# Zeros in the bias tiles: bias and maximum of a score tile by one VectorE instruction

## The chip, the cores and the metric

The kernel runs on one core of a Trainium2 chip. The metric is the time of one execution on the device, in microseconds (us). TensorE (PE) does the matrix products, and its weight loads are listed as PEld; VectorE (DVE) and ScalarE (ACT) do the elementwise work, GpSimd (POOL) some of it, and SyncE (SP) issues most of the DMA transfers. Each engine, and each engine's DMA queue, takes its instructions in order.

## The reference

One step of a two-layer transformer on 128 context tokens and 512 latent tokens, in fp32. A layer has four parallel token mixers (A to D), gates, an output projection, and a gated MLP. Branch A is the one that is changed here: neighbourhood attention with a bias for each pair of positions.

```python
bias = rpb[:, dr[:, None, :], dc[None, :, :]]
s_loc = jnp.einsum('brqhd,brkhd->bhrqk', qg, kg) * scale + bias[None]
s_loc = jnp.where(col_ok[None, None, None], s_loc, NEG_INF)
s_ctx = jnp.einsum('brqhd,blhd->bhrql', qg, k_ctx) * scale
p = jax.nn.softmax(jnp.concatenate([s_ctx, s_loc], axis=-1), axis=-1)
o = (jnp.einsum('bhrql,blhd->brqhd', p[..., :L], v_ctx)
     + jnp.einsum('bhrqk,brkhd->brqhd', p[..., L:], vg))
```

So a query's softmax runs over its local keys, with bias, and over the 128 context keys, without.

## The kernel before

Every matrix product is done with fp32 operands split into two parts, a high part `H` and the rest `L`, and three products (high by high, low by high, high by low). Weights come through SP in pieces of up to 128x1024 (`raw`), are split by ACT into `wh` (line 303) and by DVE into `wl` (line 332), and feed accumulations that are called `d`. The operands of attention are called `c` and `g` (large slots), scores and small products stand in four PSUM tiles `ps`, attention outputs in `po`, probabilities in `p`.

The program is written out by a planner (`run`, from line 438). Each step is a Python generator; the planner keeps a clock for each engine (`clk`, line 229) with a cost for each instruction, and takes the next step that its clocks call ready, by priority; when none is, it lets TensorE go on with the dense products in the fixed list `fq`. What is written out is then the fixed order in which each engine does its work. A changed cost or a missing instruction therefore moves other instructions too, on all engines, as far as the mixer part of a layer goes.

Attention of a pair of heads has two passes. `attn1` (line 1783) makes scores with queries on the partitions, only to get each query's maximum and the sum of its exponentials. `attn2` (line 1908) makes the scores again with keys on the partitions, takes the exponential and multiplies with the values. Ahead of both, `prep64` splits and transposes queries and keys ("the K split" and "the K transposes" below: `split_l` at line 1584, and the products with `identR` at line 1593 and after).

In branch A, `attn1` has for each head one tile for the context queries and four tiles `b` of 128 latent queries. The latent tile holds 128 context keys and then 256 local keys (`b` of 0 and 3) or 384 (`b` of 1 and 2). Line 1801 adds the bias to the local part and takes its maximum (on the chip two instructions, CUSTOM_DVE_ANT_0 and a read of its accumulator), line 1804 takes the maximum of the 128 context columns, line 1813 joins both and negates, and ACT takes the exponential (line 303). There are 2 layers, 2 pairs, 2 heads and 4 tiles: 32 such tiles.

The bias tiles are loaded by SP (`bias_load`, line 1777) from arrays that the host lays out (`rpb0` for `attn1`, `rpb1` for `attn2`): for each head a load of 640 columns and one of `BIAS_W[which]` columns. In both layers the `rpb0` loads of the two pairs stand among weight loads, in the first layer also among the loads of `w_ada`, whose products with the condition (line 347, `c<-c,cs,c`) DVE sums for the modulation. Queries and keys of branches B to D that were computed early are stored to DRAM (`sp`) and loaded again ahead of their preparation (`restore`, line 1171).

Of the kernel before, what the change touches and what calls it, by code (L numbers as in the profile page):

```python
# [14 lines left out]
OP = mybir.AluOpType  # L15
AX = mybir.AxisListType

DEPTH = 2
# [89 lines left out]
AB1 = 1  # L108
MGQ = 1
RING = 10  # L110
BIAS_W = (256, 640)
WPOS = 6
XPOS = ((0, 1), (2, 3), (4, 5), (6, 7))

# [74 lines left out]
def emit(nc, tc, t):  # L189
# [18 lines left out]
    class S:  # L208
# [4 lines left out]
        w = NW  # L213
# [12 lines left out]
    def free(k, n=1):  # L226
        FREE[k] += [S.cur] * n

    def clk(e, cost, port=False):
        s = max(C[e], S.cur)  # L230
        if port:
            s = max(s, C["X"])
            C["X"] = s + cost - (130 if e == "G" else 0)
        C[e] = s + cost
        S.cur = s + cost + S.t[0]
# [30 lines left out]
    def SM(cols, dt=F):  # L266
        if cols > 10:
            return sp.tile([128, 32], dt, tag="r", name=nm("r"), bufs=5)[:, :cols]
        return sp.tile([128, 10], dt, tag="s", name=nm("s"))[:, :cols]

    def SL(cols):
        return sp.tile([128, 20], F, tag="sl", name=nm("sl"), bufs=6)[:, :cols]
# [40 lines left out]
    def vec(cols, port=False):  # L313
        clk("V", 67 + 1.042 * cols, port)
# [34 lines left out]
    def vsmall(n=1):  # L349
        clk("V", 90 * n)  # L350
# [105 lines left out]
    def has(*flag):  # L456
        return lambda: flag in done
# [1313 lines left out]
    def bias_load(l, p, which):  # L1771
        yield 4
        rows = [[Q(), Q()], [Q(), Q()]]
        for h in range(2):
            c0 = 0
            for b, w in zip(rows[h], (640, BIAS_W[which])):
                nc.sync.dma_start(b[:, :w], t["rpb%d" % which][l, p, h][:, c0:c0 + w])
# [5 lines left out]
    def attn1(l, br, p, res, idx):  # L1783
        terms = res["terms"]
        band = br in "AC"
        if br == "A":
            yield has("b", l, p, 0)
            bias1 = BIAS.pop((p, 0))
        NM = SL(10).rearrange("p (h j) -> p h j", h=2)
        S2 = SL(20).rearrange("p (h j x) -> p h j x", h=2, j=5)  # L1790
        nc.vector.memset(S2, 0.0)
        sk = [nsink[:, 2 * p + h:2 * p + h + 1] for h in range(2)] if br == "C" else None
        left = [0]

        def rest(h, j, ss, n, bt):
            mc = SM(2)
            s = ss[0]
            nmx = NM[:, h, j:j + 1]
            if bt is not None:
                vec(n)  # L1800
                nc.vector.tensor_tensor_reduce(out=s[:, 128:128 + n], in0=s[:, 128:128 + n], in1=bt, scale=1.0, scalar=-3e38,
                                               op0=OP.add, op1=OP.max, accum_out=mc[:, 0:1])
                vec(128)
                nc.vector.tensor_reduce(mc[:, 1:2], s[:, 0:128], axis=AX.X, op=OP.max)
                ex = [s[:, 0:128 + n]]
            else:
                ex = [x[:, :n] for x in ss]
                for x, e in enumerate(ex):
                    vec(n)
                    nc.vector.tensor_reduce(nmx if len(ex) == 1 and sk is None else mc[:, x:x + 1], e, axis=AX.X, op=OP.max, negate=True)  # L1810
            if bt is not None:
                vsmall()
                nc.vector.tensor_scalar(nmx, mc[:, 0:1], mc[:, 1:2], -1.0, op0=OP.max, op1=OP.mult)
            elif len(ex) == 2 or sk is not None:
                vsmall()
                nc.vector.tensor_scalar(nmx, mc[:, 0:1], mc[:, 1:2] if len(ex) == 2 else sk[h], None, op0=OP.min)
            yield
            for x, e in enumerate(ex):
                act(e, e, AF.Exp, bias=nmx, accum_out=S2[:, h, j, x:x + 1])
            free("s", len(ss))  # L1820
            left[0] += 1

        for h in range(2):
            tl = terms[h]["l1"]
            for j in range(5):
                two = j > 0 and not band
                yield N(s=2 if two else 1, at=S.pe)
                ss = [PS() for _ in range(1 + two)]
                bt = None
                qs = slice(128 * j, 128 * j + 128)  # L1830

                def score(o, a, b, last=True):
                    for i, (q, k, K) in enumerate(tl):
                        mm(o, q[0:K, qs], k[0:K, a:b], i == 0, last and i == len(tl) - 1)

                if j == 0:
                    n = 128
                    score(ss[0][:, 0:128], 0, 128)
                elif two:
                    n = 320  # L1840
                    for x in range(2):
                        score(ss[x][:, 0:320], 128 + 320 * x, 448 + 320 * x)
                else:
                    b = j - 1
                    lo, hi = max(b - 1, 0), min(b + 2, 4)
                    n = 128 * (hi - lo)
                    s = ss[0]
                    if lo:
                        score(s[:, 0:128], 128, 256)
                        score(s[:, 128:128 + n], 256 + 128 * lo, 256 + 128 * hi, br == "A")  # L1850
                    else:
                        score(s[:, 0:128 + n], 128, 256 + n, br == "A")
                    if br == "A":
                        X, Y = bias1[h]
                        bt = (X[:, 0:256], X[:, 256:640], X[:, 256:640], Y[:, 0:256])[b]
                    else:
                        ms = [(kb, 2 * (kb > b)) for kb in (b - 1, b + 1) if lo <= kb < hi]
                        for kb, w in ms:
                            mm(s[:, 128 + 128 * (kb - lo):256 + 128 * (kb - lo)], identR, maskR[:, 64 * w:64 * w + 128], False, (kb, w) == ms[-1])
                        n += 128  # L1860
                spawn(rest(h, j, ss, n, bt), 2)
        yield lambda: left[0] == 10

        if br == "A":
            for row in bias1:
                rel(*row)
        lse = SM(10)
        l2 = lse.rearrange("p (h j) -> p h j", h=2)
        vsmall()
        nc.vector.tensor_tensor(l2, S2[:, :, :, 0], S2[:, :, :, 1], op=OP.add)  # L1870
        if sk is not None:
            es = SM(10)
            e2 = es.rearrange("p (h j) -> p h j", h=2)
            sr = gain(l, "sink_c")[:, 2 * p:2 * p + 2]
            for h in range(2):
                act(e2[:, h], NM[:, h], AF.Exp, bias=sr[:, h:h + 1])
            yield
            vsmall()
            nc.vector.tensor_tensor(lse, lse, es, op=OP.add)
        ln = SM(10)  # L1880
        yield
        act(ln, lse, AF.Ln)
        yield
        nl = SM(10)
        n2 = nl.rearrange("p (h j) -> p h j", h=2)
        vsmall(12)
        nc.vector.tensor_tensor(n2, NM, ln.rearrange("p (h j) -> p h j", h=2), op=OP.subtract)
        for h in range(2):
            zH, zL = LZ[:, :, 32 * h], LZ[:, :, 32 * h + 1]
            nc.vector.tensor_copy(zH, n2[:, h])  # L1890
            nc.vector.tensor_tensor(zL, n2[:, h], zH.bitcast(F), op=OP.subtract)
        yield N(s=2)
        s, s2 = PS(), PS()
        for j in range(4):
            mm(s[0:34, j * 128:(j + 1) * 128], LZ[:, j + 1], identR, True, True)
        mm(s2[0:34, 0:128], LZ[:, 0], identR, True, True)
        for h in range(2):
            q, r0 = terms[h]["lse"]
            evac(q[r0:r0 + 2, 128:640], s[32 * h:32 * h + 2, :], False)
        free("s")  # L1900
        for h in range(2):
            q, r0 = terms[h]["lse"]
            evac(q[r0:r0 + 2, 0:128], s2[32 * h:32 * h + 2, 0:128], False)
        free("s")
        yield
        done.add(("lse", l, idx))
# [263 lines left out]
def _host(x_prompt, x_sample, cache_nat_k, cache_nat_v, cache_gqa_k, cache_gqa_v, cache_win_k, cache_win_v,  # L2170
# [13 lines left out]
    vec = np.zeros((DEPTH, 128, NV), np.float32)  # L2184
    for l in range(DEPTH):
# [7 lines left out]
                                axis=1).astype(np.float32)  # L2193
# [5 lines left out]
    idx = np.arange(16)[:, None] * -1 + 15 + np.arange(48)[None, :]  # L2199
    off = 7 - np.arange(8)[:, None] + np.arange(8)[None, :]  # L2200
    lay = lambda v: v[:, :, off][..., idx].transpose(0, 1, 2, 4, 3, 5).reshape(DEPTH, 2, 2, 128, 8, 48)
    for w, seq in enumerate((((1, 1), (2, 0), (0, 0), (1, 0), (2, 0), (0, 0), (1, 2)),
                             ((1, 1), (2, 0), (0, 0), (1, 0), (2, 0), (0, 0), (1, 0), (2, 0), (0, 0), (1, 2)))):
        tb = [lay(v[..., ::-1, ::-1] if w else v) for v in pads]
        a["rpb%d" % w] = np.ascontiguousarray(np.concatenate(
            [tb[v][..., 16 * d:16 * d + 16].reshape(DEPTH, 2, 2, 128, 128) for d, v in seq], axis=-1))
    a["cos64"], a["sin64"] = _rope(64)
    a["cos32"], a["sin32"] = _rope(32)
    a["maskC"] = _masks()
# [26 lines left out]
```

## Time and profile before

| | |
|---|---|
| median of 3 runs | 2325.96 us (2325.31 to 2327.69) |
| the profiled execution: time, span | 2329.46 us, 2327.7 us |
| busy in the span | PE 98%, PEld 94%, DVE 77%, ACT 48%, POOL 13% |
| mean granted clock of TensorE | 0.991 |
| bytes moved by DMA | 292.18 MB, 126 GB/s in the mean |

The span is the time from the first to the last instruction of that execution; the time itself lies 1.8 us above it. Clocks are given as a share of full speed: 1.00 is 2.4 GHz, 0.50 is 1.2 GHz.

### The profile page before, as it was taken

How to read it: one execution, taken by the hardware profiler on the slowest of the kernel's cores; microseconds unless marked ns; L12 is line 12 of the kernel's file. 1: busy time of each engine (PE TensorE's matmuls, PEld its weight loads, DVE VectorE, ACT ScalarE, POOL GpSimd, SP SyncE). 2: the span in 40 equal slices, each digit the busy share in tenths (PEclk: the TensorE clock that was granted, in tenths of full speed). 3: DMA queues.
4: the chain of work that ended last, by engine and by line, in shares of the span. 5: the costliest groups of instructions: out<-in, count | busy, mean ns of one | idle time of the engine just before them, and what ended most of it. 6: DMA issues, size and time to landing. Idle time of an engine off the chain costs nothing.

```text
span 2327.7 us, 40730 instructions
## 1 busy us (share of the span) xinstructions
PE 2273.9 (98%) x15480; PEld 2195.2 (94%) x15480; DVE 1800.1 (77%) x3399; ACT 1125.4 (48%) x2419; POOL 300.1 (13%) x563
## 2 busy tenths in 40 slices
PE   8899999999999999999999999999999999999999
PEld 3899999999999999999999989999999999999999
DVE  5678878878779888766677788887879997565566
ACT  4467767664344323233355676666534542323232
POOL 0112112312021000000022121132111200000000
PEclk9999999999999999999999999999999999999999
DMA  7632323335554342322264332233456432221313
GB/s 255 235 122 73 112 82 110 100 127 175 196 186 137 105 155 93 125 78 68 87 202 155 121 114 82 87 111 109 145 179 225 172 114 85 85 74 59 98 51 132
DMA packets 114018, 292.18 MB, mean 126 GB/s; under 512 B 15840, under 2 KB 24736, under 8 KB 113824
## 3 DMA queue, kind: packets, MB, share of 16 engines
q1 hardware_dynamic: 105664, 258.43, 33.8%
q0 software_dynamic: 8160, 31.15, 3.6%
q8 instruction: 122, 2.00, 0.4%
q14 instruction: 72, 0.59, 0.1%
HBM read 257.59 MB, written 31.95 MB: 124 GB/s over the span
## 4 chain that ended last, share of the span: by engine, by line
PE 76%; DVE 13%; ACT 4%; DMA 3%; issue 3%; SPq 0%; POOL 0%; DVEq 0%; ACTq 0%; POOLq 0%
PE d L368 63%; PE ps L368 10%; DVE c L347 3%; PE po L368 2%; DVE wl L332 2%; DMA c<-w_ada 2%; DVE c L332 1%; ACT wh L303 1%; DVE p L347 1%; DVE hL L347 1%; DVE g L332 1%; ACT ps L303 1%; DMA g<-sp 1%; ACT c L325 1%; ACT c L303 0%
## 5 line engine op out<-in xcount | busy, mean ns | idle before, releaser
L368 PE MATMUL d<-hH,wh 128*128 128x320 f32 x2432 | 760.4, 313 | 0.4 <-ACT hH L303 0.4
L368 PE MATMUL d<-hL,wh 128*128 128x320 f32 x2432 | 754.7, 310 | 3.4 <-DVE hL L347 3.4
L368 PE MATMUL d<-hH,wl 128*128 128x320 f32 x2432 | 753.9, 310 | 0.8 <-DVE wl L332 0.8
L368 PEld LDWEIGHTS d<-hL,wh 128*128 128x128 f32 x2432 | 460.1, 189 | 7.6 <-DVE hL L347 5.0
L368 PEld LDWEIGHTS d<-hH,wh 128*128 128x128 f32 x2432 | 459.9, 189 | 4.1 <-ACT hH L303 0.7
L368 PEld LDWEIGHTS d<-hH,wl 128*128 128x128 f32 x2432 | 459.5, 189 | 1.1 <-DVE wl L332 1.1
L303 ACT ACTIVATE wh<-raw 128x1024 fp32r<-128x1024 f32 (+4 forms) x344 | 333.7, 971 | 206.2 <-PE d L368 178.4
L368 PE MATMUL d<-c,wh 128*128 128x320 f32 x1776 | 411.5, 311 | 2.8 <-DVE c L347 1.1
L332 DVE TENSOR_TENSOR wl<-raw,wh 128x1024 fp32r<-128x1024 f32 (+4 forms) x344 | 383.4, 1115 | 35.1 <-ACT wh L303 33.0
L303 ACT ACTIVATE c<-d 128x320 f32<-128x320 f32 (+2 forms) x376 | 130.7, 372 | 389.6 <-PE d L368 384.2
L368 PEld LDWEIGHTS d<-c,wh 128*128 128x128 f32 x1776 | 300.6, 189 | 7.8 <-DVE c L347 2.2
L368 PE MATMUL d<-c,wl 128*128 128x320 f32 x960 | 297.1, 309 | 0.0
L368 PE MATMUL d<-wh,hH 128*128 128x256 f32 (+1 forms) x720 | 208.7, 290 | 3.9 <-ACT wh L303 2.4
L347 DVE SCALAR_TENSOR_TENSOR c<-c,cs,c 128x512 f32<-128x512 f32 x266 | 198.0, 791 | 15.9 <-DMA c<-w_ada 15.9
L368 PE MATMUL d<-wh,hL 128*128 128x256 f32 (+1 forms) x720 | 205.1, 285 | 3.4 <-DVE hL L347 3.4
L368 PE MATMUL d<-wl,hH 128*128 128x256 f32 (+1 forms) x720 | 205.3, 285 | 1.0 <-DVE wl L332 1.0
L303 ACT ACTIVATE c<-c 128x641 f32<-128x641 f32 (+8 forms) x197 | 127.8, 665 | 161.1 <-DVE c L347 78.4
L368 PEld LDWEIGHTS d<-c,wl 128*128 128x128 f32 x960 | 180.9, 188 | 0.0
L347 DVE SCALAR_TENSOR_TENSOR c<-c,vec,c 128x641 f32<-128x641 f32 x174 | 154.6, 888 | 12.7 <-DVE c L347 0.5
L368 PE MATMUL d<-g,wh 128*128 128x320 f32 x656 | 158.9, 309 | 0.0
L1337 DVE TENSOR_SCALAR c<-c,vec 128x641 f32<-128x641 f32 x87 | 53.5, 614 | 124.7 <-ACT c L303 121.5
L368 PEld LDWEIGHTS d<-wh,hH 128*128 128x128 f32 x720 | 138.1, 192 | 5.1 <-ACT wh L303 2.6
(196 smaller groups left out, 3449.2 us busy)
## 6 DMA issues: line engine op xcount, KB each, us to landing
raw<-wst SPq DMA_DIRECT2D x264, 512.0 KB
c<-w_ada SPq DMA_DIRECT2D x184, 256.0 KB
mgd<-c POOLq DMA_DIRECT2D x46, 320.0 KB, 3.2
raw<-wst SPq DMA_DIRECT2D x32, 320.0 KB
c<-mgd SPq DMA_DIRECT2D x30, 320.0 KB
raw<-wst SPq DMA_DIRECT2D x32, 256.0 KB
c<-rpb SPq DMA_DIRECT2D x24, 320.0 KB
c<-xin SPq DMA_DIRECT2D x16, 320.0 KB
```

Source lines behind the costliest of these rows:

```text
L303: nc.scalar.activation(out, in_, func, **kw)
L325: nc.scalar.copy(out, in_)
L332: nc.vector.tensor_tensor(out, a, b, op=op)
L347: nc.vector.scalar_tensor_tensor(out, a, s, b, op0=op0, op1=op1)
L368: nc.tensor.matmul(out, lhsT, rhs, start=start, stop=stop, skip_group_check=True)
L1337: nc.vector.tensor_scalar(y[:, :641], u[:, 1:642], c[:, 1:2], c[:, 3:4], op0=OP.mult, op1=OP.add)
```

## The change

The bias tiles of `attn1` get 128 columns of zeros beside the local ones, so that one instruction covers the whole score tile, local and context columns together. The load of 256 columns becomes one of 512. In the last tile (`b` of 3) the scores are written with the local keys first, so that the bias tile's zeros lie at its end. The reduction at line 1804 goes, and the small instruction that joined two maxima only negates one. The planner is told another cost for the long instruction.

```diff
-BIAS_W = (256, 640)
+BIAS_W = (512, 640)
...
             if bt is not None:
-                vec(n)
-                nc.vector.tensor_tensor_reduce(out=s[:, 128:128 + n], in0=s[:, 128:128 + n], in1=bt, scale=1.0, scalar=-3e38,
-                                               op0=OP.add, op1=OP.max, accum_out=mc[:, 0:1])
-                vec(128)
-                nc.vector.tensor_reduce(mc[:, 1:2], s[:, 0:128], axis=AX.X, op=OP.max)
+                e = s[:, 0:128 + n]
+                clk("V", 237 + 1.042 * (n + 128))
+                nc.vector.tensor_tensor_reduce(out=e, in0=e, in1=bt, scale=1.0, scalar=-3e38, op0=OP.add, op1=OP.max,
+                                               accum_out=mc[:, 0:1])
                 ex = [s[:, 0:128 + n]]
...
             if bt is not None:
                 vsmall()
-                nc.vector.tensor_scalar(nmx, mc[:, 0:1], mc[:, 1:2], -1.0, op0=OP.max, op1=OP.mult)
+                nc.vector.tensor_scalar(nmx, mc[:, 0:1], -1.0, None, op0=OP.mult)
...
-                    if lo:
+                    if br == "A" and b == 3:
+                        score(s[:, 0:n], 256 + 128 * lo, 256 + 128 * hi, False)
+                        score(s[:, n:128 + n], 128, 256)
+                    elif lo:
                         score(s[:, 0:128], 128, 256)
                         score(s[:, 128:128 + n], 256 + 128 * lo, 256 + 128 * hi, br == "A")
...
-                        bt = (X[:, 0:256], X[:, 256:640], X[:, 256:640], Y[:, 0:256])[b]
+                        bt = (X[:, 256:640], Y[:, 0:512], Y[:, 0:512], X[:, 0:384])[b]
...
-    for w, seq in enumerate((((1, 1), (2, 0), (0, 0), (1, 0), (2, 0), (0, 0), (1, 2)),
+    for w, seq in enumerate((((0, 0), (1, 2), None, (1, 1), (2, 0), None, (0, 0), (1, 0), (2, 0)),
...
-            [tb[v][..., 16 * d:16 * d + 16].reshape(DEPTH, 2, 2, 128, 128) for d, v in seq], axis=-1))
+            [np.zeros((DEPTH, 2, 2, 128, 128), np.float32) if e is None else
+             tb[e[1]][..., 16 * e[0]:16 * e[0] + 16].reshape(DEPTH, 2, 2, 128, 128) for e in seq], axis=-1))
```

TensorE's products are the same in number and size. Their order changes in the mixer part of both layers; from the output projection to the end of the MLP it is the same as before. Three places matter below. Line numbers after the change are up to 3 higher, and buffer numbers differ.

DVE in the first layer, at the loads of `w_ada`. Before:

```order
L332 TENSOR_TENSOR wl_831<-raw_728,wh_815 128x1024
L347 SCALAR_TENSOR_TENSOR c_582<-c_585,cs,c_582 128x512
L347 SCALAR_TENSOR_TENSOR c_583<-c_585,cs,c_583 128x512
L332 TENSOR_TENSOR wl_873<-raw_744,wh_859 128x1024
L347 SCALAR_TENSOR_TENSOR c_582<-c_586,cs,c_582 128x512
L347 SCALAR_TENSOR_TENSOR c_583<-c_586,cs,c_583 128x512
```

The same place with the change:

```order
L332 TENSOR_TENSOR wl_831<-raw_731,wh_815 128x1024
L332 TENSOR_TENSOR wl_870<-raw_747,wh_859 128x1024
L347 SCALAR_TENSOR_TENSOR c_582<-c_585,cs,c_582 128x512
L347 SCALAR_TENSOR_TENSOR c_583<-c_585,cs,c_583 128x512
L347 SCALAR_TENSOR_TENSOR c_582<-c_586,cs,c_582 128x512
L347 SCALAR_TENSOR_TENSOR c_583<-c_586,cs,c_583 128x512
```

The second weight split now stands ahead of the instruction that waits for a load of `w_ada` (into `c_585`), not behind it. A copy of 128x128 (`c_545<-d_818`) also comes to DVE, right behind these rows.

DVE some ten rows later, up to the K split of the first pair (`g_1073`, with the change `g_1065`). Before:

```order
L332 TENSOR_TENSOR wl_1004<-raw_833,wh_985 128x1024
L332 TENSOR_TENSOR c_996<-c_582,c_995 128x512
L332 TENSOR_TENSOR c_998<-c_583,c_997 128x512
L332 TENSOR_TENSOR g_438<-g_438,s_993 128x640
L332 TENSOR_TENSOR g_438<-g_438,gain_428 128x640
L332 TENSOR_TENSOR g_1035<-g_546,g_1035 128x6x64
L332 TENSOR_TENSOR g_1036<-g_546,g_1036 128x6x64
L332 TENSOR_TENSOR c_437<-c_437,s_1014 128x640
L332 TENSOR_TENSOR c_437<-c_437,gain_428 128x640
L332 TENSOR_TENSOR wl_1092<-raw_875,wh_1049 128x1024
L332 TENSOR_TENSOR g_1073<-g_438,g_1073 128x6x64
```

With the change:

```order
L332 TENSOR_TENSOR wl_1000<-raw_833,wh_985 128x1024
L332 TENSOR_TENSOR g_438<-g_438,s_980 128x640
L332 TENSOR_TENSOR g_438<-g_438,gain_428 128x640
L332 TENSOR_TENSOR c_437<-c_437,s_990 128x640
L332 TENSOR_TENSOR c_437<-c_437,gain_428 128x640
L332 TENSOR_TENSOR g_1027<-g_546,g_1027 128x6x64
L332 TENSOR_TENSOR g_1028<-g_546,g_1028 128x6x64
L332 TENSOR_TENSOR wl_1084<-raw_872,wh_1043 128x1024
L332 TENSOR_TENSOR g_1065<-g_438,g_1065 128x6x64
```

The two splits of the modulation's sums (`c_996`, `c_998`) are gone from here; they stand behind the K split now.

SP in the first layer, at the second pair's `rpb1` loads and the reload of branch B's first pair (`sp`). Before:

```order
L580 DMA raw_1821<-wst 128x544
L1013 DMA g_1894<-cache_win_k 128x64
L1014 DMA g_1894<-cache_win_v 128x64
L1777 DMA c_1908<-rpb 128x640
L1777 DMA c_1909<-rpb 128x640
L1777 DMA c_1910<-rpb 128x640
L1777 DMA c_1911<-rpb 128x640
L1171 DMA c_1916<-sp_1338 128x640
L1171 DMA g_1918<-sp_1340 128x768
L580 DMA raw_1944<-wst 128x816
```

With the change:

```order
L580 DMA raw_1778<-wst 128x544
L1013 DMA g_1862<-cache_win_k 128x64
L1014 DMA g_1862<-cache_win_v 128x64
L580 DMA raw_1882<-wst 128x816
L1777 DMA c_1978<-rpb 128x640
L1777 DMA c_1979<-rpb 128x640
L1777 DMA c_1980<-rpb 128x640
L1777 DMA c_1981<-rpb 128x640
L1171 DMA c_1986<-sp_1357 128x640
L1171 DMA g_1988<-sp_1359 128x768
```

A weight load has moved ahead of these six loads. In the second layer this place has the same order as before.

## Rows read from the trace of the kernel before

**Rows 1.** The page's busy time of each engine, share of the span, instructions

```profile
PE 2273.9 (98%) x15480; PEld 2195.2 (94%) x15480; DVE 1800.1 (77%) x3399; ACT 1125.4 (48%) x2419; POOL 300.1 (13%) x563
```

**Rows 2.** Groups by form, DVE: operation, shapes, count | busy us, mean ns | idle before

```profile
L1804 DVE TENSOR_REDUCE s<-ps 128x1 f32<-128x128 f32 x32 | 9.3, 292 | 1.1
...
L1801 DVE CUSTOM_DVE_ANT_0 ps<-ps,c 128x384 f32<-128x384 f32 x16 | 8.9, 557 | 0.1
...
L1801 DVE CUSTOM_DVE_ANT_0 ps<-ps,c 128x256 f32<-128x256 f32 x16 | 6.8, 425 | 0.3 <-ACT wh L303 0.3
```

**Rows 3.** Timeline of DVE, one bias tile, first layer: start us, us, instruction [idle before]

```profile
171.76 0.56 DVE L1801 CUSTOM_DVE_ANT_0 ps<-ps,c 128x384 f32<-128x384 f32 x1
172.24 0.14 DVE L1801 DVE_READ_ACCUMULATOR2_ANT s<- 128x1 f32 x1
172.41 0.29 DVE L1804 TENSOR_REDUCE s<-ps 128x1 f32<-128x128 f32 x1
172.74 0.21 DVE L1813 TENSOR_SCALAR sl<-s 128x1 f32<-128x1 f32 x1
172.87 0.42 DVE L332 TENSOR_TENSOR p<-p,p 128x256 fp32r<-128x256 f32 x1
```

**Rows 4.** Timeline of DVE, its first idle times around 191 us

```profile
167.29 1.01 DVE L332 TENSOR_TENSOR wl<-raw,wh 128x816 fp32r<-128x816 f32 x1 [0.58 <-ACT wh L303]
...
192.99 0.69 DVE L328 CAST g<-ps 64x512 fp32r<-64x512 f32 x1 [0.57 <-ACT g L325]
```

**Rows 5.** Timeline of PE: waits in the mixer part [idle before <-releaser]

```profile
76.06 0.38 PE L368 MATMUL d<-wh,hH 128*128 128x256 f32 x1 [2.38 <-ACT wh L303]
...
77.32 0.38 PE L368 MATMUL d<-wl,hH 128*128 128x256 f32 x1 [0.76 <-DVE wl L332]
...
108.39 0.66 PE L368 MATMUL ps<-identR,g 128*128 128x128 f32 x4 [3.18 <-DVE g L332]
...
129.56 0.73 PE L368 MATMUL ps<-g,c 66*128 66x512 f32 x2 [0.41 <-ACT ps L303]
...
191.66 0.55 PE L368 MATMUL ps<-identR,g 128*128 128x128 f32 x3 [0.99 <-DVE g L332]
...
1326.12 0.66 PE L368 MATMUL ps<-identR,g 128*128 128x128 f32 x4 [0.94 <-DVE g L332]
```

**Rows 6.** Windows: us, PE busy (matmuls), granted clock, DMA share, GB/s

```profile
70.00:72.00 2.00, 2.00 (x20) 1.00 0.74 215
72.00:74.00 2.00, 1.68 (x15) 1.00 1.00 397
76.00:78.00 2.00, 1.18 (x7) 1.00 1.02 401
108.40:116.40 8.00, 8.00 (x55) 0.79 0.22 68
232.00:246.00 14.00, 12.06 (x63) 0.76 0.57 186
1366.00:1378.00 12.00, 9.54 (x53) 0.86 0.54 188
```

**Rows 7.** Timeline of SP's DMA issues, first layer: start us, us to issue

```profile
65.07 2.10 SPq L1777 DMA_DIRECT2D c<-rpb  x4
...
80.47 1.85 SPq L1777 DMA_DIRECT2D c<-rpb  x4
...
163.11 1.85 SPq L1777 DMA_DIRECT2D c<-rpb  x4
...
168.33 20.05 SPq L580 DMA_DIRECT2D raw<-wst  x2
```

**Rows 8.** Timeline of DVE, first layer, up to the K split

```profile
89.89 1.41 DVE L347 SCALAR_TENSOR_TENSOR c<-c,cs,c 128x512 f32<-128x512 f32 x2 [3.96 <-DMA c<-w_ada]
91.22 1.22 DVE L332 TENSOR_TENSOR wl<-raw,wh 128x1024 fp32r<-128x1024 f32 x1
...
101.30 1.30 DVE L332 TENSOR_TENSOR c<-c,c 128x512 fp32r<-128x512 f32 x2
...
107.78 1.02 DVE L332 TENSOR_TENSOR g<-g,g 128x384 fp32r<-128x384 f32 x2
```

## Prediction

> **What bounds the kernel now.** I read the page's busy times first: TensorE is busy for 2273.9 of 2327.7 us [rows 1]. It does the same products after the change, so all that the change can win or lose is in the other 53.8 us, and in how often the clock falls. The second view was the difference between the two programs: the order of work moves only in the mixer part of the layers, so the idle time in the norms, in the output projection and in the MLP stays. The third was the timeline of TensorE in the mixer parts, for each wait and its releaser [rows 5]. These are single waits of 0.3 to 3.2 us, most of them released by DVE. The fourth was DVE's timeline ahead of those waits, and the fifth the granted clock behind them [rows 6].
>
> DVE is busy for 77% of the span in the mean, which would say that it bounds nothing. The stage says otherwise. In the first layer DVE works without a pause from 167.29 to 191.66 [rows 4], through the eight bias tiles of the second pair, and at 191.66 TensorE has waited 0.99 for DVE's split of the next pair's keys. At 1326.12, in the second layer, the same wait is 0.94 [rows 5]. A shorter tile ends these waits sooner.
>
> **The tile.** In the timeline, one tile's long instruction and the read of its accumulator take from 171.76 to 172.41, the reduction with its wait until 172.74, and the next work starts at 172.87 [rows 3]. The change takes out 172.74 - 172.41 = 0.33. It adds 128 columns to the long instruction: 557 - 425 = 132 ns for 128 columns [rows 2]. So a tile gets 0.33 - 0.13 = 0.20 shorter, eight tiles 1.6, all 32 6.3 us of DVE. A form with 512 columns isn't in the trace; that the slope goes on is taken from the two forms that are. If the widest form cost as much more as the whole reduction (292 ns), the tile would save 0.04, which is the lower bound. The last small instruction reads one operand less; I count nothing for it. Nothing else in the step changes on ACT: the exponential has the same columns. TensorE's products for the last tile come in another order, at the same count, and cost nothing.
>
> What lies on the path is less than 6.3. At 191.66 and 1326.12 TensorE can win only what it waits there, 0.99 and 0.94, since 1.6 is more than either; after that it has work again. At 129.56 it waits 0.41 for the exponential of a bias tile of the first pair [rows 5]; three tiles stand ahead of it, worth 0.6, so 0.41 goes. In the second layer's first pair TensorE doesn't wait in this way, and its shorter tiles are worth 0. Sum of the tiles: **-2.34**.
>
> **The larger loads.** Each of the two `rpb0` groups gets 2 x 128 x 256 x 4 bytes = 262 kB more, with no more instructions on SP. The second layer has room. In the first layer the groups at 65.07 and 80.47 [rows 7] stand in a queue that is behind: from 72 to 78 us the transfers run at a share of 1.00 and about 400 GB/s [rows 6]. At 397 GB/s a group costs 0.66, at the 215 of 70 to 72 us it costs 1.22. I take 0.66 for the weights behind the first group, whose wait ends in the fast stretch. TensorE's wait ahead of 76.06 grows from 2.38 to 3.0. By itself that is not lost, because at 108.39 TensorE waits 3.18 again, for the K split [rows 5], and what it comes later it waits less there.
>
> So the start is decided by DVE's chain to the K split. It begins with a wait of 3.96 for a load of `w_ada`, at 89.89, and goes on nearly without a pause to the first half of the split at 107.78 [rows 8]. By the order shown above, one weight split of 1.2 now runs ahead of that wait, the two splits at 101.30, together 1.3, run after the chain, and a copy of 128 columns comes in, about 0.3 by the reduction of the same size [rows 2, 8]. That is -2.2. The load itself lands later by both groups: 1.3 to 2.4. The chain ends 0.9 sooner to 0.2 later; I take 0.5 sooner, since the nearer row is the faster one, but the group's own loads ran in the slower one. TensorE comes 0.66 later, so of its 3.18 a wait of 3.18 - 0.66 - 0.5 = 2.0 is left.
>
> Behind the wait of 3.18 the granted clock is 0.79 for 8 us, so part of this time ran at 1.2 GHz; that costs (1 - 0.79) x 8 = 1.68. Behind 2.38 it stays at 1.00 from 76 to 78 [rows 5, 6]. The wait that is left is nearer to 2.38, so I take the fall as gone. Sum of the start: -0.5 - 1.68 = **-2.2**. The Trainium skill (TensorE: Matmul & The Clock Gate, section HAM oscillation — how this bites in real kernels) describes a kernel that waits for a load in each step and restarts at the lower clock every time. By that rule the start would win only 0.5, and the whole 2.9 instead of 4.5. The trace agrees for the wait of 3.18 and does not for that of 2.38.
>
> **The sum** is -2.34 - 2.2 = -4.5. The profiled execution took 2329.46, which would become 2325.0; it was 3.5 above the median of the runs, so against the median of 2325.96 the forecast is **2321.4**. That is 0.2% (4.65 us), about what a measurement of this kernel can tell from no change.
>
> **The rivals.**
>
> *More goes.* The order of the mixer part is written anew, with a cost for the long instruction that fits the chip. The waits where the last input projections end, from 232 to 246 and from 1366 to 1378, may go too. In the second of these TensorE is idle for 12.00 - 9.54 = 2.46 and the clock costs 0.14 x 12 = 1.68 [rows 6]. For it: these waits are released by DVE and ACT in stages where DVE is the busier one. Against it: the same small products and the same weights meet there in any order. With one of the two gone: 2321.4 - 4.1 = 2317.3.
>
> *The clock falls all the same.* Short waits can add up: from 232 to 246 the clock is 0.76 behind waits of under a microsecond each [rows 6]. Then 1.68 of the sum stays: 2323.1. The rule named above would lead here.
>
> *Nothing is left of it.* The waits that go come back at other places, because the planner fills TensorE up to what its clocks call ready; or the wider form costs as much as what it replaces, and the change doesn't do what it says. In both: 2326.0. For it: TensorE has a dozen waits of this size in each layer's mixer part, each at another place. Against it: DVE has 6.3 us less to do in all.
>
> *Slower.* In the first layer a weight load now stands ahead of the second pair's `rpb1` loads and the reload of branch B's first pair. Before, these were issued from 163.11 on, and that weight load only at 168.33, after a wait for its buffer [rows 7]. SP takes its queue in order, so the reload would be 168.33 - 163.11 = 5.2 later. If the planner's clocks called the buffer free too soon, the K split of B is late by it: the wait of 0.99 becomes 6.2, and the clock falls, 1.68 more. With the other gains kept (-2.2 - 0.41 - 0.94) that is 5.2 + 1.7 - 3.6 = +3.3, so 2329.3, and more if the next reload is late as well. It decides once the reload is more than about 1.6, the tiles' saving, behind. Against it: TensorE has dense products to do meanwhile, and DVE has other work until 191.66.
>
> **How the numbers follow.** Forecast 0.36, within 2 us of 2321.4, so half of it on each side of 0.2%; more goes 0.17; the clock falls 0.10; nothing left 0.22, of which a few hundredths beyond 0.2% to either side, since the order is new; slower 0.15, half beyond 0.2%. Faster by over 0.2%: 0.18 + 0.17 + 0.03 = 0.38; slower 0.075 + 0.04 = 0.12; within 0.50. The range 2316.5 to 2329.5 holds all cases but the far ends of the first rival and of the last.
>
> **What would show it.** Right: a bias tile without the reduction, the 512-column form at about 0.69; waits at the K splits of branch B under 0.3 in both layers; about 3.0 ahead of the first weights behind the larger loads; under 2.3 at the first K split, and a clock of 1.00 behind it. Wrong: a form of 512 columns at 0.85 or more; a wait of several us at B's first K split, with the reload issued after 168; or the mixer parts' idle time as large as before, at other places.

## The result and the profile after

The change is slower: 2339.44 us (2338.87 to 2340.07) against 2325.72 beside it, ratio 1.0057, 95% interval 1.004 to 1.0075. Forecast was 2321.4, with a range to 2329.5. Measured once more (e15, below) the ratio was 1.0034 (1.0021 to 1.0047). So the loss is 0.3% to 0.6% by the two measurements, and its sign is certain.

The page's busy times of the changed kernel, whose span is 2338.3 us:

```profile
PE 2279.1 (97%) x15480; PEld 2201.8 (94%) x15480; DVE 1794.1 (77%) x3388; ACT 1126.2 (48%) x2397; POOL 304.8 (13%) x564
```

Against [rows 1] DVE has 6.0 us less to do, as forecast. TensorE is busy for 5.2 us more with the same 15480 products, which is time at the lower clock (its mean granted clock is 0.989, and was 0.991), and idle for 2338.3 - 2279.1 = 59.2 where it was 53.8. So of the 10.6 us between the two profiled spans half is waiting and half is the clock.

The group by form, DVE, of the tiles' long instruction:

```profile
L1802 DVE CUSTOM_DVE_ANT_0 ps<-ps,c 128x512 f32<-128x512 f32 x16 | 11.1, 693 | 0.1
L1802 DVE CUSTOM_DVE_ANT_0 ps<-ps,c 128x384 f32<-128x384 f32 x16 | 9.0, 565 | 0.0
```

The widest form takes 693 ns, where 0.69 was forecast from [rows 2]: the instruction does what it should.

TensorE's timeline in the first layer's mixer part of the changed kernel, its larger waits:

```profile
73.83 0.38 PE L368 MATMUL d<-wh,hH 128*128 128x256 f32 x1 [2.18 <-ACT wh L303]
105.41 0.66 PE L368 MATMUL ps<-identR,g 128*128 128x128 f32 x4 [1.83 <-DVE g L332]
...
230.92 0.90 PE L368 MATMUL ps<-g,c 66*128 66x320 f32 x2 [2.03 <-DVE p L332]
...
248.53 0.90 PE L368 MATMUL ps<-g,c 66*128 66x320 f32 x2 [2.13 <-ACT ps L303]
...
309.30 0.41 PE L368 MATMUL ps<-g,c 66*128 66x128 f32 x2 [1.76 <-ACT p L303]
...
331.83 0.41 PE L368 MATMUL d<-hH,wh 128*128 128x320 f32 x1 [1.43 <-ACT c L303]
...
391.34 0.41 PE L368 MATMUL d<-hH,wh 128*128 128x320 f32 x1 [1.23 <-ACT c L303]
```

The waits of [rows 5] at 129.56, 191.66 and 1326.12 have no counterpart any more, and that at 108.39 fell from 3.18 to 1.83. But between 200 and 420 us stand five waits of 1.2 to 2.1 us where the timeline of the kernel before has none above 0.81. Windows of the first layer show what that adds up to (us; busy and instructions of PE, PEld, DVE, ACT, POOL; granted clock; DMA share; GB/s). Before:

```profile
110.00:190.00 80.00, 78.63 (x613) 76.48 (x613) 63.11 (x170) 52.08 (x133) 17.55 (x22) 0.98 0.31 101
190.00:260.00 70.00, 65.32 (x449) 62.33 (x448) 57.84 (x151) 52.27 (x151) 14.33 (x18) 0.95 0.35 117
260.00:340.00 80.00, 79.00 (x509) 74.79 (x508) 68.07 (x157) 55.87 (x128) 9.96 (x14) 1.00 0.21 71
340.00:460.00 120.00, 120.00 (x860) 118.89 (x859) 101.19 (x227) 81.90 (x206) 35.15 (x36) 1.00 0.32 106
```

With the change:

```profile
110.00:190.00 80.00, 79.72 (x632) 77.44 (x630) 64.85 (x169) 52.50 (x131) 18.27 (x22) 1.00 0.33 109
190.00:260.00 70.00, 61.85 (x405) 58.64 (x404) 56.67 (x151) 50.58 (x141) 12.60 (x16) 0.90 0.32 105
260.00:340.00 80.00, 76.13 (x485) 71.36 (x484) 62.50 (x149) 55.74 (x124) 12.72 (x18) 1.00 0.21 71
340.00:460.00 120.00, 117.86 (x833) 115.98 (x832) 98.15 (x219) 78.86 (x192) 31.54 (x31) 1.00 0.30 99
```

From 110 to 190, where the bias tiles are, TensorE gains 1.1. In the next three windows it loses 3.5, 2.9 and 2.1, and the clock falls from 0.95 to 0.90 in the first of them, worth 0.05 x 70 = 3.5 (0.93 in e15, so this part differs between executions): 12.0 in all. The tiles are done by then. Less the 1.1 and the clock's 0.02 x 80 = 1.6 that were won from 110 to 190, that is 9.3. Three products that stand in the same place of both programs confirm it, the first ahead of the mixer part, the second behind it, the third behind that of the second layer. Before:

```profile
49.78 0.38 PE L368 MATMUL ps<-identF,p 2*128 2x2 f32 x2 [2.27 <-DVE p L328]
...
504.85 0.50 PE L368 MATMUL po<-p,g 128*128 128x512 f32 x1 [0.71 <-DVE p L332]
...
1777.07 0.56 PE L368 MATMUL d<-c,wh 128*128 128x320 f32 x2 [0.20 <-DVE c L347]
```

With the change:

```profile
47.76 0.38 PE L368 MATMUL ps<-identF,p 2*128 2x2 f32 x2 [2.28 <-DVE p L328]
...
512.02 0.50 PE L368 MATMUL po<-p,g 128*128 128x512 f32 x1 [0.71 <-DVE p L332]
...
1784.24 0.56 PE L368 MATMUL d<-c,wh 128*128 128x320 f32 x2 [0.23 <-DVE c L347]
```

The first product comes 2.02 sooner with no change ahead of it, the second 7.17 later: the first layer's mixer part costs 9.2 us (7.4 by the same two products in e15). From 512 to 1784 (the second layer's mixer part among it) nothing is added, and the last 3.4 of the spans' 10.6 come behind 1784, where the order is that of before.

### The profile page after: what moved, and what is told of

Its sections match the earlier page's. It is cut to its first block, busy times and chain, and to the rows that moved or that the text cites. A ratio compares the mean times of both kernels' runs of the same rounds, so it can differ in the third digit from the quotient of the medians.

```text
span 2338.3 us, 40718 instructions
## 1 busy us (share of the span) xinstructions
PE 2279.1 (97%) x15480; PEld 2201.8 (94%) x15480; DVE 1794.1 (77%) x3388; ACT 1126.2 (48%) x2397; POOL 304.8 (13%) x564
## 4 chain that ended last, share of the span: by engine, by line
PE 76%; DVE 13%; DMA 4%; ACT 3%; issue 3%; SPq 1%; POOL 0%; DVEq 0%; ACTq 0%; POOLq 0%
PE d L368 63%; PE ps L368 10%; DVE c L347 3%; DVE wl L332 3%; PE po L368 2%; DMA c<-w_ada 2%; DVE c L332 2%; DMA raw<-wst 1%; DVE p L347 1%; DVE g L332 1%; ACT wh L303 1%; DVE p L332 1%; DVE hL L347 1%; DVE s L1809 1%; DMA g<-sp 1%
## 5 line engine op out<-in xcount | busy, mean ns | idle before, releaser
L303 ACT ACTIVATE c<-d 128x320 f32<-128x320 f32 (+1 forms) x382 | 133.6, 374 | 406.6 <-PE d L368 395.4
L303 ACT ACTIVATE c<-c 128x640 fp32r<-128x640 f32 (+7 forms) x204 | 132.2, 667 | 151.8 <-DVE c L347 75.1
```

Source lines behind the costliest of these rows:

```text
L303: nc.scalar.activation(out, in_, func, **kw)
```

## The experiments

All ratios are to the kernel before on the same chip, beside the run, with the 95% interval; 0.1% is 2.3 us. "Told" is what the planner's clocks are told; the work itself is not touched by that.

| kernel | ratio | interval |
|---|---|---|
| e15 the change again | 1.0034 | 1.0021 to 1.0047 |
| e1 merged, old numbers told | 0.9995 | 0.9986 to 1.0003 |
| e2 two instructions, new numbers told | 1.0044 | 1.0032 to 1.0056 |
| e3 merged, new cost, old load size told | 1.0004 | 0.9995 to 1.0013 |
| e4 merged, old cost, new load size told | 1.0037 | 1.0023 to 1.005 |
| e5, e6 merged, cost of -133, -33 told | 1.0004, 1.0001 | 0.9996 to 1.0013, 0.9991 to 1.0011 |
| e7 merged, cost of 300, old load size told | 1.0067 | 1.0054 to 1.008 |
| e8 merged, load of 384 told | 1.0019 | 1.0011 to 1.0027 |
| e9 merged, new numbers told in layer 0 only | 1.0034 | 1.0021 to 1.0046 |
| e10 merged, new numbers told in layer 1 only | 0.9986 | 0.9978 to 0.9995 |
| e11, e17 the change, reloads by GpSimd | 1.0024, 1.0028 | 1.0014 to 1.0034, 1.0018 to 1.0038 |
| e12, e18 as e1, reloads by GpSimd | 0.9981, 0.9984 | 0.9972 to 0.999, 0.9975 to 0.9994 |
| e13 before, reloads by GpSimd | 0.999 | 0.9981 to 0.9999 |
| e14 as e10, reloads by GpSimd | 1.0004 | 0.9995 to 1.0013 |
| e16 before, larger bias loads | 0.9999 | 0.999 to 1.0007 |

**The edit or the order.** Two kernels swap the planner's numbers between before and the change. In e1 the merged instruction stands in the order of before; e2 has the two instructions in the order of the change. The edit of e1 (that of e2 is its mirror image):

```diff
-                at = dma_at(1.43 * w)
+                at = dma_at(1.43 * min(w, 640 - 384 * (b is rows[h][1] and which == 0)))
...
-                clk("V", 237 + 1.042 * (n + 128))
+                vec(n)
+                vec(128)
```

> The changed kernel, with the planner told the two costs and the load size of the kernel before. What each engine does then stands in the order of before, but for the rows that the change takes out or widens (the last bias tile's two products swapped). Theory 'order' (the one instruction is the gain that it was meant to be, the loss lies in the order that the planner wrote from the new numbers): 2321 to 2325, that is the waits of 0.99, 0.94 and 0.41 us that a shorter tile ends, less what the larger loads cost at the first K split. Rival 'the edit itself' (the wider instruction, or its larger loads in the queue that is behind at 65 to 80 us): 2337 to 2341, as the change.

> The kernel before, with two instructions to a bias tile and its small loads, with the planner told the costs and the load size of the change: the order of the change without its merged instruction. Theory 'order': 2339 to 2347, as the change or slower by up to the 6.3 us that DVE has more to do. Rival 'the edit itself': 2325 to 2329, as before.

e1 took the time of before (2328.27 against 2330.26), e2 that of the change (2339.38). The loss is the order's, and it is there without the instruction. The gain that theory 'order' forecast for e1 did not come. Its trace shows what the tiles are worth and where that goes. TensorE's timeline has no wait at B's K splits, but three new ones, which ACT ends:

```profile
176.34 0.84 PE L368 MATMUL ps<-g,c 66*128 66x128 f32 x4 [0.90 <-ACT ps L303]
...
1308.55 0.84 PE L368 MATMUL ps<-g,c 66*128 66x128 f32 x4 [1.17 <-ACT ps L303]
...
1494.54 0.73 PE L368 MATMUL ps<-g,c 66*128 66x128 f32 x4 [1.15 <-ACT p L303]
```

ACT's timeline of e1 ahead of the first of them:

```profile
173.51 0.47 ACT L303 ACTIVATE c<-g 128x320 f32<-128x320 f32 x1 [1.40 <-DMA g<-sp]
...
176.19 0.33 ACT L303 ACTIVATE ps<-ps,sl 128x128 f32<-128x128 f32 x1
```

ACT waits 1.40 for the reload of B's first pair, and the exponential that TensorE waits for stands behind it. Ahead of the other two ACT waits for reloads in the same way, 1.65 at 1305.72 and 1.47 at 1493.07. With shorter tiles everything comes sooner to this point, and the reload doesn't.

**Which number.** e3 has the first part of the diff above alone (the load size), e4 the second (the cost).

> The changed kernel, with the planner told the old size of the bias loads but the new cost of the instruction. Theory 'order', if the cost of the instruction alone is what writes the bad order: 2337 to 2343. If it takes the load size as well: 2320 to 2330. Rival 'the edit itself': 2337 to 2341.

> The changed kernel, with the planner told the old costs of the two instructions but the new size of the bias loads. Theory 'order', if the load size (which moves the work at 65 to 110 us) writes the bad order: 2337 to 2343; if only the cost of the instruction does, or both together: 2320 to 2330. Rival 'the edit itself': 2337 to 2341.

The told size of the loads makes the loss by itself (1.0037), the told cost of the instruction does not (1.0004). The real loads are innocent; in e16 they have 256 columns of zeros more and all else is as before:

> The kernel before, its order untouched; the four bias loads of 256 columns carry 512 (256 columns of zeros that nothing reads). By the prediction's step (0.66 us to a group, hidden behind the wait at the K split): within 1 us of before. If the loads hold up the first layer's start: slower than before by 1.3 to 2.4 us.

0.9999 (0.999 to 1.0007): they cost nothing that can be measured.

**Are truer numbers better, and can the planner's end clock be trusted?** Four more orders of the merged kernel, by other told numbers:

```diff
-                clk("V", 237 + 1.042 * (n + 128))
+                clk("V", -133 + 1.042 * (n + 128))
```

> The changed kernel; only the number that the planner is told for the long instruction differs, -133 + 1.042 per column in place of 237 + 1.042. Theory 'the order decides' (each number gives another order, and the planner's own clock at the last product tells which orders are good: 2291.8 for before, 2296.2 for the change, 2285.9 here): faster than before by 6 to 12 us. Rival 'true numbers make the better order' (this number lies 370 ns below what the instruction takes, so waits on DVE come that the planner doesn't see): as slow as the change, +8 to +14 over before.

> The same with -33 in place of 237; the planner's own clock ends at 2287.0. Theory 'the order decides': faster than before by 4 to 11 us. Rival 'true numbers': +8 to +14 over before.

> The changed kernel with 300 in place of 237 and the bias loads told at their old size; the planner's own clock ends at 2305.6, 13.9 later than before. Theory 'the order decides': slower than before by 12 to 25 us. Rival 'the change's loss comes from the told size of the loads alone': within 4 us of before, as the kernel with the old load size was.

> The changed kernel with the 512-column bias loads told to the planner as 384 columns, halfway between the size that kept the time and the size that lost 9 us; its own clock ends at 2301.6, 9.9 later than before. Theory 'the order decides': slower than before by 8 to 20 us, more than at either end. Rival 'the told size of the loads decides, in proportion': between the two, +2 to +7.

Each theory misses somewhere. 'The order decides', with the planner's end clock as its measure, hits at e7 and misses at e5, e6 and e8; 'true numbers' misses at e5 and e6, and 'the told size alone' at e7. A cost that is wrong by 370 ns gave the time of before, not a loss; and an end clock 5.9 sooner gave no gain. Of the two orders with a late end clock one lost 0.67%, the other 0.19%. That 0.19% lies inside the rival's +2 to +7, but not for its reason: e8 doesn't have the waits of the change in a smaller size. It has one like them (2.38 at 245.93) and a larger one of its own, at TensorE's first K split, where the other orders wait 0.7 to 3.2:

```profile
106.91 1.12 PE L368 MATMUL ps<-identR,g 128*128 128x128 f32 x4 [8.23 <-DVE g L332]
```

e5 and e6 are also told the new size of the loads, and don't have the loss; e7 is told the old size, and has the largest. So neither number is the bad one by itself. Each pair of numbers gives another order, with another set of waits; over these orders the time follows neither the numbers' truth nor the planner's end.

**Which layer.** e9 and e10 tell the new numbers in one layer, by a condition on `l` around the lines of the first diff.

> The changed kernel with the planner's new numbers in the first layer only; the second layer's mixer part has the order of before. The trace of the change shows its added waits from 200 to 420 us, in the first layer: slower than before by 7 to 13 us, nearly the whole loss. Rival 'both layers' (each pays for its new order): 3 to 6 us.

> The changed kernel with the planner's new numbers in the second layer only; the first layer's mixer part has the order of before. If the loss is the first layer's: within 3 us of before. Rival 'both layers': slower by 3 to 6 us.

The whole loss is the first layer's (1.0034, as e15); in the second the new order was, if anything, better (0.9986). The last line of the windows 190 to 260, 260 to 340 and 340 to 460, first e9's, then e10's:

```profile
sum 270.00, PE 254.80 PEld 244.98 DVE 214.84 ACT 182.58 POOL 54.21; mean PE 84.93 PEld 81.66 DVE 71.61 ACT 60.86 POOL 18.07
```

```profile
sum 270.00, PE 265.20 PEld 256.97 DVE 227.69 ACT 191.12 POOL 59.40; mean PE 88.40 PEld 85.66 DVE 75.90 ACT 63.71 POOL 19.80
```

TensorE is idle there for 15.2 us in the one and 4.8 in the other.

**What the new waits wait for.** In the changed kernel's chain of waits the one at 309.30 goes back to a reload (start us, us, what):

```profile
299.19 1.15 DVE wl L332
...
300.36 0.33 SPq L580
...
301.25 5.89 DMA g<-sp
...
307.17 1.10 ACT c L303 x2
308.26 0.41 ACT g L303
308.68 0.49 ACT p L303
...
309.30 0.41 PE ps L368 x2
```

SP waits with a weight load until DVE's split has freed the buffer, then issues the reload of branch C's second pair, and ACT and TensorE wait for its landing. In e11, with the change's order on PE, DVE and ACT, GpSimd issues the reloads:

```diff
-            nc.sync.dma_start(x[:, :cols], d)
+            nc.gpsimd.dma_start(x[:, :cols], d)
```

> The changed kernel with its own order on every engine; the reloads of branches B to D are issued by GpSimd's queue, where they stand behind no weight load. Theory 'late reloads' (the weight loads ahead of them on SP's queue make them late, as in the rival 'Slower' of the prediction): the waits at 309.30 (1.76) and the like go and with them the stretch behind: 5 to 10 us faster than the change. Rival 'chains' (the new waits are chains of ACT, DVE and TensorE, and the reloads are only one of them): 0 to 3 us faster than the change, with the waits at 230.92 and 248.53 still there.

> The change itself, beside the others on one chip: slower than before by 0.4% to 0.65% (9 to 15 us). Its counterpart with the reloads by GpSimd was 0.24% slower, so the reloads in SP's queue are worth 4 to 9 us of it.

> The change with the reloads by GpSimd's queue, again. If the reloads in SP's queue are a part of the change's loss: 0.1% to 0.3% slower than before, as the first time. If the first time was scatter: 0.34% or more.

In e11 GpSimd issues this reload at 291.42, ten us sooner, and between 296 and 335 TensorE has one wait left:

```profile
329.29 0.41 PE L368 MATMUL d<-hH,wh 128*128 128x320 f32 x1 [1.43 <-ACT c L303]
```

So the wait at 309.30 is the reload's, and the rest is not: 2.02 and 2.13 are still there, at 231.53 and 247.97. Yet ACT waited for this reload before, too. There SP issued it at 301.51, and TensorE waited only 0.49 behind it. ACT's timeline and TensorE's of the kernel before:

```profile
307.53 0.47 ACT L303 ACTIVATE c<-g 128x320 f32<-128x320 f32 x1 [1.51 <-DMA g<-sp]
...
309.58 0.62 PE L368 MATMUL ps<-g,c 66*128 66x384 f32 x2 [0.49 <-ACT p L303]
```

From its issue to ACT's start on it took 6.0 us before and 5.9 with the change, and from there to TensorE's product 2.1 in both. But TensorE had other work for 7.6 us from the issue on before, and has it for 6.3 with the change (6.3 in e15 too). So what the order took away is work behind the reload. By time the reloads are 1.0034 - 1.0028 to 1.0034 - 1.0024, 1.4 to 2.3 us of the loss; the intervals overlap, so this size is not settled (against the first measurement's 1.0057 it would be 6.8 to 7.7 us; e15 lost less than the 0.4% to 0.65% expected of it). "Chains" holds by the waits that are left, and by the first layer, between the two products at 49.78 and 504.85 above: 455.1 us before, 464.3 and 462.5 with the change, 460.5 and 464.6 in e11 and e17. The two largest of these waits, by the changed kernel's trace alone: at 230.92 TensorE waits for a product of DVE, at 248.53 for an exponential of ACT, and each stands behind the split of a weight. DVE's timeline, then ACT's:

```profile
229.18 1.22 DVE L332 TENSOR_TENSOR wl<-raw,wh 128x1024 fp32r<-128x1024 f32 x1
230.32 0.55 DVE L332 TENSOR_TENSOR p<-ps,c 128x384 f32<-128x384 f32 x1
```

```profile
246.46 1.05 ACT L303 ACTIVATE wh<-raw 128x1024 fp32r<-128x1024 f32 x1
...
248.03 0.33 ACT L303 ACTIVATE ps<-ps,sl 128x128 f32<-128x128 f32 x1
```

Another, in its chain of waits:

```profile
328.52 1.28 ACT L303
329.82 0.21 ACT s L303
330.05 1.28 ACT L303
331.34 0.45 ACT c L303
331.83 2.90 PE d L368 x18
```

ACT changes its table (1.28), takes one small function, changes back, and only then empties the accumulator that the next dense product needs. In the kernel before ACT's timeline has the same two table loads, and TensorE does not wait behind them:

```profile
328.01 1.28 ACT L303 ACT_TABLE_LOAD   x1
...
330.31 1.28 ACT L303 ACT_TABLE_LOAD   x1
```

So again nobody is busy for longer; with the change the dense work that should cover it stands behind it on TensorE.

**A better version.** e12 is e1 with the reloads by GpSimd, e13 the kernel before with them, e14 adds the second layer's new order.

> The merged instruction in the order of before, with the reloads issued by GpSimd's queue. In the trace of that order with SP's reloads, the shorter tiles bring TensorE sooner to waits of 0.90 and 1.17 for an exponential that stands on ACT behind a reload. If these are what eats the tiles' saving: 2 to 4 us faster than before, so the best of all. If not: within 2 us of before.

> The merged instruction in the old order with the reloads by GpSimd's queue, again. If it beats the kernel before: 0.1% to 0.3% faster, as the first time. If the first time was scatter: within 0.1%, as the combination.

> The kernel before, with two instructions to a tile; only its reloads are issued by GpSimd's queue in place of SP's. If the merged instruction is the gain of its counterpart (0.19% faster than before): within 2 us of before. If the reload is: 3 to 5 us faster than before, and the merged instruction is worth nothing.

> The merged instruction, the planner's new numbers in the second layer only, reloads by GpSimd's queue. If the two gains (0.14% and 0.19% faster than before, of which the merged instruction itself is in both) add up: 5 to 8 us faster than before. If the second layer's gain was the same waits as the reloads': 3 to 5 us faster.

e12 beats both kernels, twice (2326.03 and 2326.63 against 2329.66 and 2329.25). The three waits of e1 are gone from its trace. Of its 0.16% to 0.19% the reloads alone are 0.10% (e13), and the merged instruction the other 0.06% to 0.09%, 1.4 to 2.1 us; the two intervals overlap that of e13, so this split is a best estimate. The second layer's gain did not add to it: e14 misses both of its expectations, no run shows why, and whether e10's 0.14% is more than its scatter is open.

## Why the prediction was wrong

**The tile: right.** 693 ns, 6.0 us of DVE, and the three waits of 0.99, 0.94 and 0.41 gone. They stay in kernels with two instructions (0.98 at B's K split in e13 and in e16) and are absent from e1 and e12. The term of 2.34 is 1.4 to 2.1 in time once no reload stands behind the tiles, and about 1.2 with a bound through zero in e1, where the waits of 0.90, 1.17 and 1.15 take its place. What is late next was the question to ask there, and the prediction asked it of the split alone.

**The larger loads: not seen.** Forecast was a wait of 3.0 ahead of the first weights; it was 2.18, and 2.39 in e16, against 2.38. The 0.66 to a group does not show; but this wait is 1.73 in e11 and 3.66 in e17, which are one program, so single executions can't tell 0.66 from nothing.

**The start: right in the wait, not in the clock.** The wait at the first K split is 1.83, and 1.79 in e15, where 2.0 was forecast. Over all profiles it is 0.70 to 1.83 in the seven with the change's order up to there, and 1.96 to 3.18 in the eight with that of before (2.01 and 2.93 in e12 and e18, one program). The windows behind it, the change's first and e15's second:

```profile
105.40:113.40 8.00, 7.99 (x56) 7.99 (x56) 4.80 (x10) 2.82 (x6) 0.00 (x0) 0.79 0.21 68
```

```profile
106.20:114.20 8.00, 7.96 (x68) 7.96 (x69) 5.67 (x13) 4.20 (x8) 0.00 (x0) 1.00 0.19 68
```

The same program, the same wait, and the clock falls once and once not. The longer wait that the prediction compared with, the one ahead of the first weights, is no better guide. It is 2.38 in the kernel before and 2.39 in e16, which has its order; the 8 us behind it, before first:

```profile
76.06:84.06 8.00, 7.24 (x59) 7.04 (x60) 6.06 (x7) 3.48 (x6) 0.00 (x0) 1.00 1.04 406
```

```profile
76.73:84.73 8.00, 7.24 (x46) 7.03 (x47) 6.07 (x7) 3.51 (x6) 0.00 (x0) 0.79 1.04 407
```

So 1.68 could not be booked as gone from the wait's length, as I did. At the first K split the granted clock of the 8 us behind the wait was 0.79 or less in all eleven profiles with a wait of 1.96 to 8.23, the forecast's 2.0 among them, in two of the six with 1.70 to 1.83, and 1.00 in the three with 0.70 to 1.47. The Trainium skill (TensorE: Matmul & The Clock Gate, section HAM oscillation — how this bites in real kernels) has a kernel restart at the lower clock after every wait for a load; its waits are of about 3 to 5 us. The traces agree for the waits at the first K split that are as long, 3.14 and more. By that section waits of about 2 us would not do it, so the prediction took it further than it goes, both against the 2.38 and for the rival with 2.0; and here the clock fell behind 1.96 and 2.39 (e16) all the same, so the measurement decides.

**The step that failed:** the sum has no term for the waits that the new order makes at other places. Of the order it prices two places on DVE, ahead of 110 us; the place in SP's queue stands in the rival "Slower", and all others in "Nothing is left of it", where the waits that come back add up to about what they were, with a few hundredths for more than 0.2%. In their place the runs show five new waits of 1.2 to 2.1 us, 7 to 9 us in the first layer, which come with the order and without the instruction (e2) and go with the old numbers (e1). The instruction, which the forecast priced well, moved 2 us by the best estimate above; the orders tried with the merged instruction moved the time from -0.14% to +0.67%. "More goes" had the sign wrong in the first layer: the stage from 232 to 246 became a part of the worst window, 190 to 260.

**"Slower" had half of the mechanism and missed the place.** ACT and TensorE do wait for a reload that SP issues behind a weight load, but not for that of B's first pair, which went out at 164.57 (165.05 before): it was C's second pair, 1.76 at 309.30. That this one was made late, as the rival has it, is not shown: counted from the product at 49.78 (47.76 with the change, 48.07 in e15) it was issued 1.8 later in one profile of the change and 0.4 sooner in the other. TensorE had less work left behind it, and it is a small part of the loss.

**Not shown to be the change's:** the 3.4 us behind 1784, in an unchanged order. From the product there to the end it is 550.6 us before, and 554.1 and 554.2 in the two profiles of the change. In the 18 profiles with this order behind it, it is 549.3 (e8) to 554.8 (e14), and 550.9 and 552.9 in e12 and e18, one program. From 1800 to 1900 and from 1900 to 1980 the clock is 0.97 and 0.96 with the change, in e15 too, and 0.98 and 0.98 before; that is 1.0 + 1.6 of it. Why it falls more often there, and why both profiles of the change lie high, I did not find.

## What to carry to other kernels

Where a planner or a scheduler rewrites the order, an edit has two effects, and they can be timed apart: keep the edit and give the planner the old numbers, then keep the old code and give it the new ones. Here, with TensorE 98% busy, the second effect was larger than the first (7 to 9 us against 2), and neither truer costs nor a better end on the planner's own clock made the order good. And ask of every wait that is removed what its engine reaches sooner: here a reload, which had to be moved to another queue before the shorter tile was worth anything that could be measured.

## What I had not expected of the hardware

From the issue of the reload of B's first pair at 164.46 to ACT's start on it at 173.51 it took 9.1 us in e1, behind the four `rpb1` loads issued from 162.02; that of C's second pair landed after 5.89 in the changed kernel. And the clock behind one and the same wait was 0.79 in one execution and 1.00 in another, with 1.8 us at the first K split and with 2.4 us ahead of the first weights.
